# A pooling layer's norms: mean-and-variance instruction per half, residual added on VectorE, residual rows and weight splits in other places

## The chip, the cores and the metric

One core of a Trainium2 chip runs the whole network in one launch. The metric is the device time of one execution in microseconds. TensorE does the matmuls, ScalarE (ACT) and VectorE (DVE) the elementwise work, GpSimd (POOL) here only powers of single columns, SyncE (SP) issues the transfers of weights. Each engine works its own instructions in the order in which they stand, and waits for the others by semaphores.

## What is computed

A two-layer transformer block is followed by a second block, on 256 tokens of width 1024. Layer 0 is attention, layer 1 a pooling mixer; each is followed by a layer norm, a gated feed-forward and another layer norm. The change lies where layer 0 ends and layer 1 begins:

```python
def multiscale_pool(h, w_pool, pool_scale):
    ...                                   # windowed means over 2, 4, 8, 16 tokens, minus h
    pooled = jnp.stack(outs, axis=2).astype(h.dtype)
    y = jnp.einsum('bsgi,gio->bsgo', pooled, w_pool).reshape(B, S, D)
    return y * pool_scale
...
        hx = modulate(x, sh1, sc1)
        ...
            y_lat = multiscale_pool(hx, pool_w[p], pool_scale[p])
        x = layer_norm(ALPHA * x + g1 * y_lat, ln_g[i, 0], ln_b[i, 0])
        x = layer_norm(ALPHA * x + g2 * swiglu(modulate(x, sh2, sc2), ffn_w_in[i], ffn_w_out[i]),
                       ln_g[i, 1], ln_b[i, 1])
```

## The kernel before

The 256 tokens are two halves, t = 0 and 1, of 128 rows each. Weights come as blocks of 128 x 1024 values in a fixed plan. SyncE loads up to 11 blocks ahead. For a precise product each block is split: ScalarE writes `hi`, the block rounded (L285), VectorE writes `lo`, what is left (L291), and TensorE does three matmuls, hi by the high part of the activations `xTh`, lo by `xTh`, hi by the low part `xTl` (L376 to L378). Eight `hi`/`lo` pairs can be held; `st.step(n)` splits up to n blocks of the plan where it stands, as long as seven are not yet passed, `st.pump()` as many as fit. The two blocks `PW` of the pooling weights are used whole.

The order is that of the program text; no scheduler moves anything. Around the pooling layer it runs so:

- `ffn(0, ...)` ends with the output product of half 0 and `ac0(0)`, then `mid_pool`, then the output product of half 1 and `ac0(1)`. `ac0` calls `ln_out`: VectorE multiplies the product by a row and adds the residual `xa` (L871, L872, sums taken along), ScalarE squares for the variance (L875), VectorE takes the power's argument (L418), GpSimd the power (L420), and VectorE writes the pooling input `hx` (L894, L898). `pooled` (L1119) multiplies by the window matrix; `keep(KW["a"])` puts five filler matmuls (L216) between its two token halves.
- `mid_pool` and later `ln_norm` normalise the rows on ScalarE (L905), and `next_xa` makes from them the next residual `xa` on VectorE (L910, L912).
- `res(t)` adds `xa` into PSUM by two matmuls with the identity (L1159), before the pool product for half 0, after it for half 1. `pool_mm` is the product with `PW` (L1186).
- `ln_core(0)`: ScalarE copies the sum out of PSUM with its row sum (L880), squares (L882), VectorE normalises (L890); `next_xa(1)` stands in between. `tr_evac` transposes (L722), ScalarE scales (`tev`, L745) and writes `xTh` (L425), VectorE `xTl` (L426).
- `ln_core(1)` follows, then layer 1's feed-forward. Its first chunk takes blocks G0 to G3 for both halves' gate and U0 to U3 for the other factor. TensorE does G for half 0, then U for half 0; after the sixth of U's eight steps come the transposes of half 1, then the rest.

`PS = (2, 2, 3, 3)` says how many blocks are taken at four places: in `mid_pool` (both are `PW`), after the pooled sums are copied out, before `tr_evac` and after it.

## Time and profile before

| | |
|---|---|
| median of 3 runs | 1149.41 us (1147.62 to 1149.92) |
| the profiled execution's own time | 1149.09 us |
| its span, first to last instruction | 1147.2 us |
| TensorE busy | 1110.0 us (97%) |
| VectorE, ScalarE, GpSimd busy | 759.9, 557.4, 22.6 us |
| TensorE's granted clock, mean | 0.996 of 2.4 GHz |
| the stage of the change | about 420 to 455 us |

A busy TensorE here mostly means matmuls that follow each other without a gap. What a change is worth is read at the places where TensorE stands: its timeline shows a gap in brackets with the engine that ended it, and the timelines of the other engines show what that engine did meanwhile.

### The profile page before, as it was taken

Reading aid. Unit: us, or ns where it says so; the run is one execution under the profiler, and the core shown is the slowest. Engines: PE = TensorE matmul, PEld = TensorE weight load, DVE = VectorE, ACT = ScalarE, POOL = GpSimd, SP = SyncE. Lnnn points to the kernel's source line nnn. Section 1 sums busy time; section 2 is a strip of 40 time slices with the busy share of each in tenths; the row PEclk is TensorE's granted clock in tenths of the full one; section 3 lists DMA queues with packets and bytes.
Section 4 is the critical chain, followed back from the end, with each engine's and each line's share of the span. In section 5 each row is a group of like instructions: output and inputs, shape, how many; then the busy total and the mean of one; then the engine's idle time right before and its main releaser. Section 6 shows DMA issues by size and latency. Waiting matters only on the chain.

```text
span 1147.2 us, 14156 instructions
## 1 busy us (share of the span) xinstructions
PE 1110.0 (97%) x5186; PEld 880.4 (77%) x5186; DVE 759.9 (66%) x1114; ACT 557.4 (49%) x913; POOL 22.6 (2%) x35
## 2 busy tenths in 40 slices
PE   7999888999999999999999999999999999999998
PEld 3578665678888776888888688887778877888887
DVE  7984967669986865577455865545636776555465
ACT  3452456454444427534443765557226355445353
POOL 0000000000000000000000110000000000000000
PEclk9999999999999999999999999999999999999999
DMA  9973741569997926568464654553434646464611
GB/s 360 359 261 116 275 147 60 195 233 372 343 419 280 332 79 220 191 215 303 168 225 146 224 196 147 189 193 126 169 108 146 208 147 210 162 212 164 207 38 37
DMA packets 65922, 234.62 MB, mean 205 GB/s; under 512 B 7323, under 2 KB 8347, under 8 KB 65852
## 3 DMA queue, kind: packets, MB, share of 16 engines
q1 hardware_dynamic: 64080, 227.97, 55.9%
q10 hardware_dynamic: 1772, 5.74, 1.5%
q8 instruction: 41, 0.67, 0.2%
q14 instruction: 29, 0.24, 0.1%
HBM read 232.63 MB, written 1.05 MB: 204 GB/s over the span
## 4 chain that ended last, share of the span: by engine, by line
PE 79%; DVE 10%; ACT 4%; issue 3%; DMA 2%; POOL 0%; SPq 0%; ACTq 0%; POOLq 0%; DVEq 0%
PE mm L378 16%; PE mm L376 16%; PE mm L377 16%; PE big L390 12%; PE big L392 6%; DVE lo L291 3%; DMA raw<-in_dram 2%; DVE junkb L526 2%; DVE raw L269 1%; PE big L384 1%; DVE st L666 1%; PE big L404 1%; PE big L405 1%; PE big L403 1%; PE tr L981 1%
## 5 line engine op out<-in xcount | busy, mean ns | idle before, releaser
L291 DVE TENSOR_TENSOR lo<-raw,hi 128x1024 fp32r<-128x1024 f32 x316 | 374.5, 1221 | 133.1 <-ACT hi L285 129.6
L285 ACT ACTIVATE hi<-raw 128x1024 fp32r<-128x1024 f32 x316 | 321.5, 1056 | 70.7 <-PE mm L378 52.2
L376 PE MATMUL mm<-hi,xTh 128*128 128x512 f32 (+1 forms) x872 | 337.6, 387 | 2.8 <-ACT xTh L425 2.7
L377 PE MATMUL mm<-lo,xTh 128*128 128x512 f32 (+1 forms) x872 | 331.8, 380 | 2.0 <-DVE lo L291 1.3
L378 PE MATMUL mm<-hi,xTl 128*128 128x512 f32 (+1 forms) x872 | 332.2, 381 | 0.6 <-DVE xTl L738 0.4
L376 PEld LDWEIGHTS mm<-hi,xTh 128*128 128x128 f32 x872 | 164.1, 188 | 38.4 <-ACT xTh L425 4.6
L378 PEld LDWEIGHTS mm<-hi,xTl 128*128 128x128 f32 x872 | 164.0, 188 | 34.1 <-DVE xTl L426 1.9
L377 PEld LDWEIGHTS mm<-lo,xTh 128*128 128x128 f32 x872 | 164.2, 188 | 33.4 <-DVE lo L291 3.6
L269 DVE SCALAR_TENSOR_TENSOR raw<-raw,crow 128x1024 f32<-128x1024 f32 x80 | 96.8, 1219 | 0.0
L390 PE MATMUL big<-hi,hh 128*128 128x512 f32 x256 | 80.6, 396 | 0.0
L390 PE MATMUL big<-lo,hh 128*128 128x512 f32 x256 | 79.2, 391 | 0.0
L392 PE MATMUL big<-hi,hl 128*128 128x512 f32 x256 | 79.0, 390 | 0.0
L425 ACT ACTIVATE hh<-tr 128x512 fp32r<-128x512 f32 (+1 forms) x40 | 22.9, 575 | 89.6 <-PE tr L981 49.2
L961 ACT ACTIVATE h<-mm 128x512 f32<-128x512 f32 (+1 forms) x24 | 13.5, 561 | 91.6 <-PE mm L378 91.6
L392 PEld LDWEIGHTS big<-hi,hl 128*128 128x128 f32 x256 | 48.0, 188 | 10.3
L390 PEld LDWEIGHTS big<-lo,hh 128*128 128x128 f32 x256 | 48.0, 188 | 10.3
L426 DVE TENSOR_TENSOR hl<-tr,hh 128x512 fp32r<-128x512 f32 (+1 forms) x40 | 26.3, 662 | 44.0 <-ACT hh L425 43.2
L390 PEld LDWEIGHTS big<-hi,hh 128*128 128x128 f32 x256 | 46.7, 188 | 8.6
L420 POOL TENSOR_TENSOR st<-st,half 128x4 f32<-128x4 f32 (+1 forms) x28 | 21.7, 776 | 1029.0 <-DVE st L418 1015.9
L1607 DVE TENSOR_TENSOR h<-h 128x512 f32<-128x512 f32 x16 | 11.0, 689 | 33.8 <-ACT h L1606 33.7
L1606 ACT ACTIVATE h<-mm 128x512 f32<-128x512 f32 x16 | 9.6, 598 | 39.8 <-PE mm L378 39.8
L667 ACT ACTIVATE p<-big,st 128x512 f32<-128x512 f32 x16 | 11.0, 689 | 31.4 <-DVE st L666 31.4
(316 smaller groups left out, 1256.2 us busy)
## 6 DMA issues: line engine op xcount, KB each, us to landing
raw<-in_dram SPq DMA_DIRECT2D x426, 512.0 KB, 5.0
row<-in_dram ACTq DMA_DIRECT2D x8, 512.0 KB, 6.2
tok<-in_dram SPq DMA_DIRECT2D x8, 256.0 KB, 8.0
xa<-in_dram SPq DMA_DIRECT2D x2, 512.0 KB, 6.6
out_dram<-sg SPq DMA_DIRECT2D x3, 256.0 KB, 2.0
pmat<-in_dram ACTq DMA_DIRECT2D x1, 544.0 KB
crow<-in_dram ACTq DMA_DIRECT2D x1, 512.0 KB, 6.4
out_dram<-sg SPq DMA_DIRECT2D x2, 128.0 KB, 1.7
```

The source lines that it names most:

```text
L269: V.scalar_tensor_tensor(raw, raw, 1.0, crow, op0=OP.mult, op1=OP.mult, accum_out=mc[l][:, nb:nb + 1])
L285: A.activation(hi, raw, AF.Copy)
L291: V.tensor_tensor(lo, raw, hi.bitcast(F32), op=OP.subtract)
L376: TE.matmul(ps, h, hi[:, sl], start=s, stop=False)
L377: TE.matmul(ps, h, lo[:, sl], start=False, stop=False)
L378: TE.matmul(ps, l, hi[:, sl], start=False, stop=e)
L390: TE.matmul(halves[f], h, w[:, f * 512:(f + 1) * 512], start=first and b == 0, stop=False)
L392: TE.matmul(halves[f], l, hi[:, f * 512:(f + 1) * 512], start=False, stop=last)
L420: G.tensor_tensor(r, v, half_e[:, :w], op=OP.pow)
L425: A.activation(dh, ps, AF.Copy)
L426: V.tensor_tensor(dl, ps, dh.bitcast(F32), op=OP.subtract)
L526: V.scalar_tensor_tensor(junk, raws[b], 1.0, crow if s_ else ccrow, op0=OP.mult, op1=OP.mult, accum_out=acc[2 * s_ + b])
```

## The change

- In `ac0(1)`, `ln_bn` takes the place of `ln_out`'s sums and square: after multiply and add, BN_STATS on each 512 columns and one BN_AGGR give mean and variance on VectorE. The filler is three matmuls instead of five.
- `res` is gone. VectorE adds `xa` while it reads the pool product from PSUM: for half 0 in `ln_bn(0)`, for half 1 in `ln_p` (with sums, the square still on ScalarE). ScalarE's copy with a row sum (L880) and its normalising pass (`ln_norm`, L905) are gone.
- The residual rows come from `xa_two`: two VectorE steps from the unnormalised rows, mean and power, with the two rows scaled by ALPHA on ScalarE beforehand (in `mid_gb`). Half 0's stand after the pooled sums are copied out, half 1's after the transposes of half 0.
- `PS = (3, 0, 2, 0)`: `mid_pool` splits G0; `hi_only(3)` has ScalarE write the high parts of G1 to G3 after the pooled sums are copied out, and `lo_only(1)` puts VectorE's part of each at three places: in the power's wait, after the first and after the second transposed half of half 0. The three transfers that follow are issued after the third. U0 and U1 are split before `ln_core(1)`, U2 and U3 after it.
- The normalising step of half 0 is done in two halves of 512 columns, each transposed by itself; of the scaling of four transposed columns two are on ScalarE and two on VectorE. Three of the four pooled sums are copied out by ScalarE.

```diff
-PS = (2, 2, 3, 3)
+PS = (3, 0, 2, 0)
-KW = dict(a=5, b=0, c=0)
+KW = dict(a=3, b=0, c=0)
...
+        def hi_only(self, n):
+            for _ in range(n):
+                it, raw = self.take()
+                self.split(it[1], raw, (0,))
+                self.pend.append((it[1], raw, self.his))
+
+        def lo_only(self, n):
+            for _ in range(n):
+                key, raw, self.his = self.pend.pop(0)
+                self.split(key, raw, (1,))
+                if not self.pend:
+                    self.dma()
...
     def ln_p(t, ps):
-        A.activation(s[t], ps, AF.Identity, accum_out=sm[:, 0:1])
-        V.tensor_scalar(sm[:, 1:2], sm[:, 0:1], -1.0 / D, None, op0=OP.mult)
+        for f in range(2):
+            V.scalar_tensor_tensor(s[t][:, fs], ps[:, fs], 1.0, xa[t][:, fs], op0=OP.mult, op1=OP.add,
+                                   accum_out=sm[:, f:f + 1])
+        V.tensor_scalar(sm[:, 1:2], sm[:, 0:1], sm[:, 1:2], -1.0 / D, op0=OP.add, op1=OP.mult)
         A.activation(ps, s[t], AF.Square, bias=sm[:, 1:2], accum_out=sm[:, 2:3])
+    def ln_bn(t, ps, grow=None):
+        b6 = bp.t([P, 2, 6], "bn6", bufs=2)
+        for f in range(2):
+            if grow is None:
+                V.tensor_tensor(s[t][:, fs], ps[:, fs], xa[t][:, fs], op=OP.add)
+            else:
+                V.tensor_tensor(s[t][:, fs], ps[:, fs], grow[:, fs], op=OP.mult)
+                V.tensor_tensor(s[t][:, fs], s[t][:, fs], xa[t][:, fs], op=OP.add)
+            V.bn_stats(out=b6[:, f], in_=s[t][:, fs])
+        V.bn_aggr(out=mv_[:, 0:2], in_=b6)
+    def xa_two(t, mean, r, rows, op, part):
+        if part == 0:
+            V.scalar_tensor_tensor(xa[t], s[t], mean, rows[0], op0=op, op1=OP.mult)
+        else:
+            V.scalar_tensor_tensor(xa[t], xa[t], r, rows[1], op0=OP.mult, op1=OP.add)
...
     def mid_gb():
+        for r in nx["rows"][:2]:
+            A.activation(r, r, AF.Copy, scale=ALPHA)
...
     def mid_pool():
-        ln_norm(0, mrs[0])
-        next_xa(0, nx["rows"])
         st.step(PS[0])
...
-    res(0)
-            if g % 2 == 0:
+            if g != 1:
                 A.activation(dst, pv, AF.Copy)
-    st.step(PS[1])
-    ln_norm(1, mrs[1])
-    cur["rows"] = ln_rows(2, ALPHA)
+    st.hi_only(3)
+    for part in range(2):
+        xa_pool(0, part)
     pps.append(big())
...
     pool_mm(0)
     pool_mm(1)
-    ln_core(0, pps[0], None, lambda: next_xa(1, rows1))
-    res(1)
+    m0 = ln_bn(0, pps[0])
+    r0 = rstd(m0[:, 1:2], 1, LN_EPS, 1)
+    st.lo_only(1)
+    for f in range(2):
+        V.tensor_scalar(s[0][:, fs], s[0][:, fs], m0[:, 0:1], r0, op0=OP.subtract, op1=OP.mult)
+    for f in range(2):
+        tr_half(s[0][:, 512 * f:512 * f + 512], f, 0, xTh, xTl, cur["cols"], fp, act_t=(0, 1))
+        st.lo_only(1)
     st.done(("PW", 0), ("PW", 1))
+    for part in range(2):
+        xa_pool(1, part)
+    cur["rows"] = ln_rows(2, ALPHA)
     st.step(PS[2])
-    tr_evac(s[0], 0, xTh, xTl, cur["cols"], fp)
-    st.step(PS[3])
     ln_core(1, pps[1], None)
```

On VectorE, from the normalising step of half 0 (L890 before) to the fourth U block, the order before was this. The `lo` rows are G2, G3, U0, then U1, U2, then U3; L881 to the second L890 is the layer norm of half 1:

```order
L890 TENSOR_SCALAR s_1326<-s_1326,st_816_3560,st_818_3568 128x1024 [waits Pool_49]
L291 TENSOR_TENSOR lo_3575<-raw_3257,hi_3573 128x1024 [waits DMAHW1_49,Activation_49]
L291 TENSOR_TENSOR lo_3581<-raw_3263,hi_3579 128x1024 [waits DMAHW2_49,Activation_49]
L291 TENSOR_TENSOR lo_3587<-raw_3266,hi_3585 128x1024 [waits DMAHW3_49,Activation_49]
L426 TENSOR_TENSOR xTl_71<-tev_3596,xTh_70 128x4x128 [waits Activation_49]
L426 TENSOR_TENSOR xTl_71<-tev_3608,xTh_70 128x4x128 [waits Activation_49]
L291 TENSOR_TENSOR lo_3617<-raw_3272,hi_3615 128x1024 [waits DMAHW4_49,Activation_49]
L291 TENSOR_TENSOR lo_3623<-raw_3275,hi_3621 128x1024 [waits DMAHW5_49,Activation_49]
L881 TENSOR_SCALAR st_838_3627<-st_838_3627 128x1 [waits Activation_49]
L418 TENSOR_SCALAR st_839_3631<-st_838_3627 128x1 [waits Activation_49]
L890 TENSOR_SCALAR s_1326<-s_1326,st_838_3627,st_840_3633 128x1024 [waits Pool_49]
L291 TENSOR_TENSOR lo_3684<-raw_3281,hi_3682 128x1024 [waits DMAHW6_49,Activation_49]
```

And in the changed kernel, from the lo of G3 to that of U3 (L293 is a lo, L920 and L922 the residual of half 1, L898 to L929 the layer norm of half 1):

```order
L293 TENSOR_TENSOR lo_3591<-raw_3265,hi_3529 128x1024 [waits DMAHW2_49]
L920 SCALAR_TENSOR_TENSOR xa_1325<-s_1326,st_803_3501,row_2512 128x1024
L922 SCALAR_TENSOR_TENSOR xa_1325<-xa_1325,st_805_3505,row_2514 128x1024 [waits DVE_49]
L293 TENSOR_TENSOR lo_3607<-raw_3268,hi_3605 128x1024 [waits DMAHW3_49,Activation_49]
L293 TENSOR_TENSOR lo_3613<-raw_3274,hi_3611 128x1024 [waits DMAHW4_49,Activation_49]
L898 SCALAR_TENSOR_TENSOR s_1326,st_835_3617<-big_3533,xa_1325 128x512 [waits DVE_49]
L898 SCALAR_TENSOR_TENSOR s_1326,st_835_3617<-big_3533,xa_1325 128x512
L900 TENSOR_SCALAR st_835_3617<-st_835_3617 128x1 [waits DVE_49]
L434 TENSOR_SCALAR st_836_3622<-st_835_3617 128x1 [waits Activation_49]
L929 TENSOR_SCALAR s_1326<-s_1326,st_835_3617,st_837_3624 128x1024 [waits Pool_49]
L293 TENSOR_TENSOR lo_3629<-raw_3277,hi_3627 128x1024 [waits DMAHW5_49,Activation_49]
L293 TENSOR_TENSOR lo_3681<-raw_3283,hi_3679 128x1024 [waits DMAHW6_49,Activation_49]
```

The residual steps and two splits now stand ahead of that layer norm, and the lo of U2 stands behind its normalising step instead of ahead of it.

On TensorE, the matmuls on U2 for half 0 (the 37th to the 42nd of the feed-forward) and the first transpose of half 1, before:

```order
L376 MATMUL mm_3663<-hi_3621,xTh_70 128x512 [waits Activation_49]
L377 MATMUL mm_3663<-lo_3623,xTh_70 128x512 [waits DVE_49]
L378 MATMUL mm_3663<-hi_3621,xTl_71 128x512
L376 MATMUL mm_3663<-hi_3621,xTh_70 128x512
L377 MATMUL mm_3663<-lo_3623,xTh_70 128x512
L378 MATMUL mm_3663<-hi_3621,xTl_71 128x512
L722 MATMUL tr_3688<-cst_72,s_1326 128x128 [waits DVE_49]
```

and now:

```order
L392 MATMUL mm_3660<-hi_3627,xTh_70 128x512 [waits Activation_49]
L393 MATMUL mm_3660<-lo_3629,xTh_70 128x512 [waits DVE_49]
L394 MATMUL mm_3660<-hi_3627,xTl_71 128x512
L392 MATMUL mm_3660<-hi_3627,xTh_70 128x512
L393 MATMUL mm_3660<-lo_3629,xTh_70 128x512
L394 MATMUL mm_3660<-hi_3627,xTl_71 128x512
L738 MATMUL tr_3685<-cst_72,s_1326 128x128 x4
```

The waits for U2's two parts stand at the same matmuls; the transposes no longer have a wait of their own, since the lo that was waited for stands behind the normalising step.

On VectorE around the pool product's statistics, the order before, from the last copied pooled sum to the normalising step:

```order
L1170 COPY pw_805_3519<-big_3478 128x512 [waits Activation_49]
L291 TENSOR_TENSOR lo_3526<-raw_3196,hi_3524 128x1024 [waits DMAHW7_49,Activation_49]
L291 TENSOR_TENSOR lo_3532<-raw_3254,hi_3530 128x1024 [waits DMAHW0_49,Activation_49]
L904 TENSOR_TENSOR st_812_3536<-st_800_3493,st_802_3503 128x1
L881 TENSOR_SCALAR st_816_3560<-st_816_3560 128x1 [waits Activation_49]
L910 SCALAR_TENSOR_TENSOR xa_1325<-s_1326,row_2512 128x1024
L912 SCALAR_TENSOR_TENSOR xa_1325<-row_2514,xa_1325 128x1024 [waits DVE_49]
L418 TENSOR_SCALAR st_817_3566<-st_816_3560 128x1 [waits Activation_49]
L890 TENSOR_SCALAR s_1326<-s_1326,st_816_3560,st_818_3568 128x1024 [waits Pool_49]
```

And now, from the first residual step of half 0 to the first scaled column of half 0:

```order
L920 SCALAR_TENSOR_TENSOR xa_1325<-s_1326,st_790_3407,row_2512 128x1024
L922 SCALAR_TENSOR_TENSOR xa_1325<-xa_1325,st_792_3417,row_2514 128x1024 [waits DVE_49]
L909 TENSOR_TENSOR s_1326<-big_3518,xa_1325 128x512 [waits DVE_49,PE_49]
L913 BN_STATS bn_813_3550<-s_1326 128x6 [waits DVE_49]
L909 TENSOR_TENSOR s_1326<-big_3518,xa_1325 128x512
L913 BN_STATS bn_813_3550<-s_1326 128x6 [waits DVE_49]
L915 BN_AGGR st_814_3555<-bn_813_3550 128x2 [waits DVE_49]
L434 TENSOR_SCALAR st_815_3557<-st_814_3555 128x1 [waits DVE_49]
L293 TENSOR_TENSOR lo_3561<-raw_3256,hi_3525 128x1024 [waits DMAHW0_49,Activation_49]
L1242 TENSOR_SCALAR s_1326<-s_1326,st_814_3555,st_816_3559 128x512 [waits Pool_49]
L1242 TENSOR_SCALAR s_1326<-s_1326,st_814_3555,st_816_3559 128x512
L763 TENSOR_SCALAR tev_3570<-tr_3565,Gc_3302,Bc_3303 128x128 [waits PE_49,Activation_49]
```

The sums and squares that L881 and L418 waited for on ScalarE are VectorE's own (L909 to L915); G0's and G1's splits are out of the stretch ahead, and one lo stands in the power's wait.

## Rows read from the trace of the kernel before

**Rows 1.** Busy time by stretch, from 455 us on.
```profile
455.00:1147.00 692.00, 683.37 (x3244) 558.98 (x3244) 407.58 (x528) 341.04 (x543) 15.03 (x20) 1.00 0.50 171
```

**Rows 2.** TensorE timeline: start us, us, engine, line, operation, count, [idle before <- releaser].
```profile
421.79 4.46 PE L216 MATMUL tr<-crow 128*128 128x512 f32 x10
426.14 1.19 PE L1119 MATMUL mm<-pmat,pw 128*128 128x136 f32 x8
...
428.10 1.88 PE L1159 MATMUL big<-xa,cst 128*128 128x512 f32 x4
429.81 7.07 PE L1186 MATMUL big<-raw,pw 128*128 128x256 f32 x32
...
439.11 1.04 PE L722 MATMUL tr<-cst,s 128*128 128x128 f32 x8
441.97 0.50 PE L376 MATMUL mm<-hi,xTh 128*128 128x512 f32 x1 [1.82 <-ACT xTh L425]
...
442.89 0.50 PE L378 MATMUL mm<-hi,xTl 128*128 128x512 f32 x1 [0.20 <-DVE xTl L426]
...
452.12 1.03 PE L722 MATMUL tr<-cst,s 128*128 128x128 f32 x8
...
454.97 0.50 PE L376 MATMUL mm<-hi,xTh 128*128 128x512 f32 x1 [0.45 <-ACT xTh L425]
```

**Rows 3.** VectorE timeline, same columns.
```profile
417.26 1.23 DVE L910 SCALAR_TENSOR_TENSOR xa<-s,row 128x1024 f32<-128x1024 f32 x1 [1.39 <-ACT s L905]
...
420.14 0.69 DVE L871 TENSOR_TENSOR s<-big,row 128x512 f32<-128x512 f32 x1 [0.39 <-PE big L405]
420.86 0.69 DVE L872 SCALAR_TENSOR_TENSOR s<-s,xa 128x512 f32<-128x512 f32 x1
...
425.33 1.41 DVE L898 SCALAR_TENSOR_TENSOR pw<-pw,st,row 128x512 f32<-128x512 f32 x2 [0.72 <-POOL st L420]
...
436.01 1.22 DVE L912 SCALAR_TENSOR_TENSOR xa<-row,xa 128x1024 f32<-128x1024 f32 x1
437.15 0.15 DVE L418 TENSOR_SCALAR st<-st 128x1 f32<-128x1 f32 x1
438.02 0.81 DVE L890 TENSOR_SCALAR s<-s,st,st 128x1024 f32<-128x1024 f32 x1 [0.72 <-POOL st L420]
438.75 3.49 DVE L291 TENSOR_TENSOR lo<-raw,hi 128x1024 fp32r<-128x1024 f32 x3
442.15 0.69 DVE L426 TENSOR_TENSOR xTl<-tev,xTh 128x512 fp32r<-128x512 f32 x1
...
444.95 2.36 DVE L291 TENSOR_TENSOR lo<-raw,hi 128x1024 fp32r<-128x1024 f32 x2 [0.26 <-ACT hi L285]
...
449.50 0.81 DVE L890 TENSOR_SCALAR s<-s,st,st 128x1024 f32<-128x1024 f32 x1 [0.66 <-POOL st L420]
```

**Rows 4.** ScalarE timeline, same columns, from two windows.
```profile
366.73 0.60 ACT L425 ACTIVATE hh<-tr 128x512 fp32r<-128x512 f32 x1 [2.23 <-PE tr L981]
...
439.75 1.50 ACT L745 ACTIVATE tev<-tr,Bc,Gc 128x128 f32<-128x128 f32 x4 [0.79 <-PE tr L722]
441.28 0.63 ACT L425 ACTIVATE xTh<-tev 128x512 fp32r<-128x512 f32 x1
...
447.41 1.12 ACT L882 ACTIVATE big<-s,st 128x1024 f32<-128x1024 f32 x1 [0.55 <-DVE st L881]
```

**Rows 5.** Groups by line and shape: count | busy us, mean ns | idle before.
```profile
L1340 DVE SCALAR_TENSOR_TENSOR sc<-c2d,tr 128x128 f32<-128x128 f32 x8 | 1.8, 281 | 0.1
```

**Rows 6.** Stretches: us, engines' busy us, TensorE's granted clock, DMA share, GB/s.
```profile
410.00:420.00 10.00, 10.00 (x46) 8.29 (x45) 7.56 (x13) 2.49 (x3) 0.54 (x1) 1.00 0.00 1
155.80:159.50 3.70, 0.03 (x2) 0.02 (x1) 3.42 (x11) 1.21 (x3) 1.02 (x1) 1.00 0.75 247
160.70:164.20 3.50, 3.50 (x14) 2.68 (x16) 1.70 (x5) 2.77 (x8) 0.00 (x0) 0.51 0.70 275
86.00:89.00 3.00, 2.86 (x9) 2.50 (x10) 3.00 (x4) 1.54 (x2) 0.00 (x0) 0.50 0.80 289
```

More of the change, by code (lines that the diff above doesn't have):

```diff
@@ L246, in __init__ @@
             self.raws, self.tiles = {}, {}
+            self.pend = []
             self.mods_done = set()
@@ L265, in emit @@
         def emit(self):
+            assert not self.pend
             it, raw = self.take()
@@ L294, in split @@
             assert self.nw <= self.ndone + R, key
+        def hi_only(self, n):
+            for _ in range(n):
+                it, raw = self.take()
+                assert it[0] == "w" and not is32(it[1])
+                self.split(it[1], raw, (0,))
[6 more added lines that the diff above has]
+                    self.dma()
         def prescale(self, key, raw=None):
@@ L717, in body, with tr_half @@
     o32 = bp.t([P, 4, T], "pw0")
-    def tr_half(src, f, t, dh, dl, cols=None, pool=None, scalars=None, f32=False):
+    def tr_half(src, f, t, dh, dl, cols=None, pool=None, scalars=None, f32=False, act_t=ACT_T):
         ps = trt()
@@ L743, in tr_half @@
             k = 4 * f + j
-            if j in ACT_T:
+            if j in act_t:
                 A.activation(tmp[:, j], pv[:, j], AF.Identity, scale=gc[:, k:k + 1], bias=bc[:, k:k + 1])
@@ L900, in ln_out @@
         return sm[:, 1:2], r
-    def ln_norm(t, mr):
-        nmr = small(1)
-        V.tensor_tensor(nmr, mr[0], mr[1], op=OP.mult)
-        A.activation(s[t], s[t], AF.Identity, scale=mr[1], bias=nmr)
     def next_xa(t, rows, parts=(0, 1)):
@@ L1123, in f, with xa_pool @@
         def f(ps):
-            if t == 1:
-                pooled(0, range(8))
-                keep(KW["a"])
-            mrs[t] = ln_out(t, ps, nx["g2"], hx[t], nx["G"], nx["B"],
-                            lambda f: pooled(1, range(4 * f, 4 * f + 4)) if t == 1 else None)
-        return f
+            if t == 0:
+                mrs[0] = ln_out(0, ps, nx["g2"], hx[0], nx["G"], nx["B"]) + (OP.add,)
+                return
+            pooled(0, range(8))
+            keep(KW["a"])
+            m = ln_bn(1, ps, nx["g2"])
+            r = rstd(m[:, 1:2], 1, LN_EPS, 1)
+            V.scalar_tensor_tensor(hx[1], s[1], m[:, 0:1], nx["G"], op0=OP.subtract, op1=OP.mult)
+            for f in range(2):
+                fs = slice(f * 512, f * 512 + 512)
+                V.scalar_tensor_tensor(hx[1][:, fs], hx[1][:, fs], r, nx["B"][:, fs], op0=OP.mult, op1=OP.add)
+                pooled(1, range(4 * f, 4 * f + 4))
+            mrs[1] = (m[:, 0:1], r, OP.subtract)
+        return f
+    def xa_pool(t, part):
+        mean, r, op = mrs[t]
+        xa_two(t, mean, r, nx["rows"], op, part)
     def mid_pool():
-        ln_norm(0, mrs[0])
-        next_xa(0, nx["rows"])
         st.step(PS[0])
@@ L1154, in body @@
     pps = [big()]
-    def res(t):
-        for f in range(2):
-            fs = slice(f * 512, f * 512 + 512)
-            TE.matmul(pps[t][:, fs], ident, xa[t][:, fs], start=t == 0, stop=t == 1, skip_group_check=True)
-    res(0)
     p32 = [bp.t([P, 4, T], f"pw{i}") for i in range(2)]
@@ L1172, in body @@
             split_evac(pv, xTh[:, 2 * g:2 * g + 2], xTl[:, 2 * g:2 * g + 2])
-    st.step(PS[1])
-    ln_norm(1, mrs[1])
-    rows1 = nx["rows"]
-    cur["rows"] = ln_rows(2, ALPHA)
-    cur["cols"] = nx["cols"]
+    st.hi_only(3)
+    for part in range(2):
+        xa_pool(0, part)
     pps.append(big())
@@ L1186, in pool_mm @@
                     TE.matmul(pps[t][:, g * T:(g + 1) * T], p32[g // 2][:, g % 2 * 2 + k, t * P:(t + 1) * P], w[:, o_:o_ + T],
-                              start=t == 1 and g % 2 == 0 and k == 0, stop=t == 0 and k == 1, skip_group_check=True)
+                              start=k == 0, stop=k == 1)
                 continue
@@ L1199, in body @@
     pool_mm(1)
-    ln_core(0, pps[0], None, lambda: next_xa(1, rows1))
-    res(1)
+    m0 = ln_bn(0, pps[0])
+    r0 = rstd(m0[:, 1:2], 1, LN_EPS, 1)
+    st.lo_only(1)
+    for f in range(2):
+        fs = slice(f * 512, f * 512 + 512)
+        V.tensor_scalar(s[0][:, fs], s[0][:, fs], m0[:, 0:1], r0, op0=OP.subtract, op1=OP.mult)
+    cur["cols"] = nx["cols"]
+    for f in range(2):
+        tr_half(s[0][:, 512 * f:512 * f + 512], f, 0, xTh, xTl, cur["cols"], fp, act_t=(0, 1))
+        st.lo_only(1)
     keep(KW["b"])
     st.done(("PW", 0), ("PW", 1))
+    for part in range(2):
+        xa_pool(1, part)
+    cur["rows"] = ln_rows(2, ALPHA)
     st.step(PS[2])
-    tr_evac(s[0], 0, xTh, xTl, cur["cols"], fp)
-    st.step(PS[3])
     ln_core(1, pps[1], None)
```

4 lines of the change are left out of this document (added).

## The prediction

> **What bounds the kernel now.** I read the stages first (busy time by stretch), then TensorE's timeline from 420 to 455 us, then VectorE's and ScalarE's over the same stretch, each time looking for the wait that ends last. From 455 us to the end TensorE is busy 683.37 of 692 us [rows 1]: a delay that exists at 455 us stays to the end, and so does a gain. So the change is worth whatever it does to one instant, the matmul at 454.97 us with which the first feed-forward chunk of layer 1 turns to token half 1 [rows 2]. In what follows G0 to G3 and U0 to U3 are the eight weight blocks of that chunk; a block needs a high part from ScalarE and a low part ("lo") from VectorE, and TensorE takes it with six matmuls for each token half. 40 of these matmuls lie between 442.89 and 452.12 us [rows 2], 0.231 us each.
>
> What is to be seen in the rows before the change: TensorE stands between 440 and 441.97 us for the transposed rows of half 0, and hardly afterwards. It asks for the lo of U2 (its 38th matmul) at 442.89 + 35 x 0.231 = 451.0 us, and VectorE has had it since 444.95 + 2.36 = 447.3 us [rows 2, 3]. VectorE did U1 and U2 before the last steps of half 1's layer norm, whose normalising step is at 449.50 us. That is 3.7 us of slack, and it is what I think the change spends.
>
> **The change part by part.** Times are on the clock of the trace. "Dependent" VectorE instructions of 512 columns start 0.72 us apart (420.14 and 420.86), independent ones 0.66 (two in 1.41, the later one lasting 0.75); a lo takes 3.49 / 3 = 1.16 [rows 3].
>
> *Costing nothing.* Scaling two rows by ALPHA on ScalarE (two passes of 1024 columns, at most 1.12 us each as the square) lies in the 2.23 us that ScalarE idles before 366.73 us [rows 4]; without that cover it would push back the evacuation that follows by 2.2 us. The split of G0 takes the place of the old normalising pass and residual row of half 0, in the idle time around 417.26 us [rows 3]. The late issue of three weight transfers (after the third lo) hides too: the queue is idle from 410 to 420 us, with the eleven blocks ahead landed [rows 6]. The wait for the first later block is on the pooled matmuls, which come sooner. Shortening the filler matmuls (4.46 us for ten pieces, now six pieces) gives nothing: TensorE then waits longer for the same VectorE result.
>
> *Statistics of half 1 in the last layer norm of layer 0.* VectorE now does per half: multiply, add, BN_STATS, then BN_AGGR and the small step. BN_STATS has no row. Ends: 0.40 us (a single-operand pass of 1024 columns takes 0.81 [rows 3], half of it) and 1.22 us (a 1024-column pass, as if it read twice [rows 3]). I take 0.69, one pass of 512, since it reads 512 numbers as the add in front of it does. 420.14 + 4.26 (six instructions, one of them independent, five dependent) + 0.4 (two small ones) + 1.28 (the first write of the pooling input) = 426.05 us where the scaling started at 425.33 before [rows 3]: **0.7 us late**. The old square on ScalarE was hidden by that first write, so taking it away returns nothing.
>
> *Pooling.* The second set of pooled matmuls starts at 426.14 + 0.7 = 426.85 and is done 1.96 later, 428.8 [rows 2]. The residual matmuls (1.88 us) no longer stand ahead of the pool product, so this starts at 428.8 instead of 429.81 us. Its first half, 7.07 / 2, ends at 432.4: **1.0 us early** [rows 2]. VectorE is free by then: copying one pooled group (from about 428) and the two residual steps of half 0 (1.22 each [rows 3]) end near 431.1.
>
> *Statistics of half 0.* The order shows one wait on TensorE for both halves, so the adds start at 432.5: 2.8 (add, BN_STATS, add, BN_STATS) + 0.35 (two small) = 435.7; the lo of G1 (1.16) covers the power on GpSimd (437.15 to 438.02 before, 0.87 [rows 3]) and ends at 436.85; two normalising halves 0.81 [rows 3] end at 437.25 and 437.65. The transposes start at 437.35 instead of 439.11 [rows 2], and 0.64 later ScalarE evacuates two of four columns (half of 1.50 [rows 4], 438.8). VectorE's two columns wait for ScalarE's (its wait list in the order shows it), about 0.28 each by a 128-column row [rows 5]: 439.35; xTh 0.63 [rows 4]: 440.0. The feed-forward's first matmul is at about **440.05 instead of 441.97**, its third at 440.75 instead of 442.89. That gain is 1.9 to 2.1 us and holds only while blocks keep coming.
>
> *The queue behind it.* VectorE is in order. After xTl of half 0 (0.69 [rows 3], to 440.65) stand: lo G2, 441.8; two columns, 442.3; xTh of half 1, 442.95; xTl, 443.6; lo G3, 444.75; two residual steps of half 1 (1.22 each), 447.15; lo U0, **448.3**. TensorE asks for it at 440.75 + 23 x 0.231 = 446.05: 2.2 us of wait, and the early start is spent. Then lo U1, 449.45; two adds with sums, 450.85; a small one, 451.05; the square on ScalarE (1.12 [rows 4], with its sum 1.3), 452.35; the power, 453.2; normalise 0.81, 454.0; and only then **lo U2, 455.2**. TensorE asks for it at 448.3 + 12 x 0.231 = 451.1 and waits 4.1 us. ScalarE is behind in the same way: the high part of U2 now stands behind the square. Five more matmuls, and the transposes of half 1 start at 455.2 + 5 x 0.231 = 456.35 instead of 452.12 [rows 2]: **4.2 us late**. From there to the matmul that stood at 454.97 nothing changes: U3's lo is there at 456.4, and the transposed rows take as long as before.
>
> *The clock.* After TensorE stood from 155.80 to 159.50 us (0.03 of 3.70 busy), the granted clock was 0.51 from 160.70 to 164.20, and 0.50 again from 86.00 to 89.00 [rows 6], that is 1.2 of 2.4 GHz. The stretch from 451.1 to 455.2 holds one matmul. If the clock falls behind it, the rows at half speed last about 3.3 us, of which some 2.4 fall on work that runs: 1.2 us lost. Ends: 0 and half of 3.5, 1.75. A fall before the first matmul at 440.05 (only transposes from 435.9 on) would be taken up by the wait for U0.
>
> Sum: 4.2 + 1.2 = 5.4 us. The profiled execution took 1149.09 us (a span of 1147.2 and 1.9 around it), the median of the runs is 1149.41; so 1154.5 on the first and **1154.8 us** on the second. BN_STATS at its ends moves this by 4 x (0.40 - 0.69) = -1.2 and 4 x (1.22 - 0.69) = +2.1.
>
> One rule speaks for a little less. The rows show a dependent pair 0.06 us further apart than an independent one [rows 3]. The Trainium skill, page "VectorE: DVE Perf Modes", section "The DRAIN you can't avoid", states that a semaphore between two VectorE instructions costs nothing extra. By it the eight dependent hand-overs in the two statistics chains would give back 0.5 us, 1154.3; by the rows the sum stands, and I keep it.
>
> **The rivals.**
> *The clock holds.* Only the 4.2 us: **1153.6 us**. For it: between 440 and 441.97 us TensorE also stood, and the matmuls behind ran at their old spacing [rows 2]. Against it: the new stand is twice as long.
> *VectorE gets there sooner (no change).* If the adds of half 0 may start when the first half of the pool product is written (1.8 us sooner) and BN_STATS costs 0.40, the lo of U2 comes at 452.2: +1.2 and no fall of the clock, **1150.6 us**. Against it: the order gives the second add no wait of its own, so the first one's wait covers both.
> *Faster: the early start is kept.* The chain through the pool lost 1.88 us of residual matmuls and ScalarE's two passes over the rows, and the feed-forward starts 1.9 us sooner (3.1 with BN_STATS at its low end): **1146.3 to 1147.5 us**. It decides if the lo of U2 is there by 440.75 + 35 x 0.231 = 448.8 us, so VectorE would have to need 6.4 us less than I add up between 432.5 and 455.2; no single row is that far off.
> *The change does not do what it says* is excluded for the order (it is built so), and open for BN_STATS alone: at 1.22 it gives 1156.9.
>
> **How the numbers follow.** Clock falls, 1154.8: 0.45. Clock holds, 1153.6: 0.30. No change, 1150.6: 0.14. Faster, 1146.9: 0.11. Within 0.2% (about what a measurement of this kernel can tell from no change) is 1147.1 to 1151.7. Faster 0.11, same 0.14, slower 0.75. The likeliest's own range is 1153.6 to 1156.9. For 8 in 10 the range reaches down through the no-change case to 1150.0 and up to 1157.5 (BN_STATS dear and the clock loss 1.75); outside are the faster case and some 0.08 at the two ends.
>
> **What would show it.** Right, on TensorE's timeline: the first matmul of layer 1's feed-forward about 2 us earlier, a wait of about 2 us on a lo after 25 matmuls, one of about 4 us on a lo after 37, transposes of half 1 about 4 us later, and the same spacing from there to the end; on VectorE: the normalising step of half 1 ahead of U2's lo; in the clock of the stretches behind 454 us: 0.5 for some 3 us. Wrong: BN_STATS far from 0.69 us; no wait on U2; a later stage that gives the 4 us back; or TensorE's work between 420 and 455 us ending sooner than 455.

## The result and the profile after

The changed kernel takes **1162.59 us** (median of 4 runs, 1161.51 to 1163.23) against 1149.66 us before in the same session: ratio 1.0114 (95% interval 1.0101 to 1.0127), some 13 us slower. The forecast was 1154.8 us with a range up to 1157.5: right in sign, too small by more than half. The profiled execution has a span of 1160.0 us.

VectorE's timeline after, first. Columns in all timelines: start us, duration us, engine, line, operation, out<-in, shapes, count, [idle before <- releaser].

```profile
423.52 0.69 DVE L913 BATCH_NORM_STATS2 bn<-s 128x6 f32<-128x512 f32 x1
424.25 0.21 DVE L915 BATCH_NORM_AGGREGATE st<-bn 128x2 f32<-128x12 f32 x1
424.50 0.15 DVE L434 TENSOR_SCALAR st<-st 128x1 f32<-128x1 f32 x1
424.57 1.27 DVE L1167 SCALAR_TENSOR_TENSOR pw<-s,st,row 128x1024 f32<-128x1024 f32 x1
426.28 1.42 DVE L1170 SCALAR_TENSOR_TENSOR pw<-pw,st,row 128x512 f32<-128x512 f32 x2 [0.44 <-POOL st L436]
...
432.70 0.69 DVE L909 TENSOR_TENSOR s<-big,xa 128x512 f32<-128x512 f32 x1 [1.18 <-PE big L1223]
433.42 0.69 DVE L913 BATCH_NORM_STATS2 bn<-s 128x6 f32<-128x512 f32 x1
434.03 0.67 DVE L909 TENSOR_TENSOR s<-big,xa 128x512 f32<-128x512 f32 x1
...
435.71 0.15 DVE L434 TENSOR_SCALAR st<-st 128x1 f32<-128x1 f32 x1
435.79 1.23 DVE L293 TENSOR_TENSOR lo<-raw,hi 128x1024 fp32r<-128x1024 f32 x1
437.45 1.00 DVE L1242 TENSOR_SCALAR s<-s,st,st 128x512 f32<-128x512 f32 x2 [0.43 <-POOL st L436]
...
446.04 1.28 DVE L920 SCALAR_TENSOR_TENSOR xa<-s,st,row 128x1024 f32<-128x1024 f32 x1
447.36 1.28 DVE L922 SCALAR_TENSOR_TENSOR xa<-xa,st,row 128x1024 f32<-128x1024 f32 x1
448.56 2.35 DVE L293 TENSOR_TENSOR lo<-raw,hi 128x1024 fp32r<-128x1024 f32 x2
...
454.63 0.81 DVE L929 TENSOR_SCALAR s<-s,st,st 128x1024 f32<-128x1024 f32 x1 [0.72 <-POOL st L436]
455.36 2.35 DVE L293 TENSOR_TENSOR lo<-raw,hi 128x1024 fp32r<-128x1024 f32 x2
```

This is the queue as the prediction had laid it out: the residual passes of half 1 (446.04, 447.36) stand ahead of the lo of U0 and U1, and the lo of U2 comes behind half 1's normalising step, where before it was done 2.2 us ahead of it (444.95 + 2.36 against 449.50) [rows 3]. The waits of 0.44 and 0.43 us for GpSimd (426.28, 437.45) stand where before had 0.72 each [rows 3]; the forecast had hidden both behind work on VectorE, and they come back below.

TensorE's timeline after, and what ScalarE does ahead of U2's high part (the row 453.63). They answer to [rows 2, 4].

```profile
421.68 2.74 PE L216 MATMUL tr<-crow 128*128 128x512 f32 x6
427.08 1.19 PE L1155 MATMUL mm<-pmat,pw 128*128 128x136 f32 x8 [2.66 <-DVE pw L1170]
...
429.04 7.07 PE L1223 MATMUL big<-raw,pw 128*128 128x256 f32 x32
438.06 1.20 PE L738 MATMUL tr<-cst,s 128*128 128x128 f32 x8 [1.94 <-DVE s L1242]
441.09 0.79 PE L392 MATMUL mm<-hi,xTh 128*128 128x512 f32 x1 [1.84 <-ACT xTh L441]
...
449.83 0.50 PE L393 MATMUL mm<-lo,xTh 128*128 128x512 f32 x1 [0.60 <-DVE lo L293]
...
454.72 0.51 PE L392 MATMUL mm<-hi,xTh 128*128 128x512 f32 x1 [2.08 <-ACT hi L287]
456.63 0.80 PE L393 MATMUL mm<-lo,xTh 128*128 128x512 f32 x1 [1.41 <-DVE lo L293]
...
458.93 1.91 PE L738 MATMUL tr<-cst,s 128*128 128x128 f32 x8
```
```profile
452.48 1.12 ACT L901 ACTIVATE big<-s,st 128x1024 f32<-128x1024 f32 x1 [5.94 <-DVE st L900]
...
453.63 1.04 ACT L287 ACTIVATE hi<-raw 128x1024 fp32r<-128x1024 f32 x1
```

Feed-forward starts a little sooner, then TensorE waits at U0's lo, 3.5 us at U2 (first for the high part, which stands behind the square on ScalarE, then for the lo), and the transposes of half 1 come late. The rows 449.83 and 456.63 are the two forecast waits. The granted clock in the stretches around (window, length, busy us of PE, PEld, DVE, ACT, POOL, then PEclk, DMA share, GB/s; as [rows 6]):

```profile
440.00:444.00 4.00, 2.91 (x7) 2.29 (x8) 2.79 (x6) 1.69 (x4) 0.00 (x0) 0.50 0.25 83
...
446.00:450.00 4.00, 3.40 (x16) 2.50 (x15) 3.96 (x5) 0.54 (x1) 0.00 (x0) 1.00 0.99 331
450.00:456.00 6.00, 3.15 (x12) 2.00 (x12) 3.87 (x9) 3.52 (x5) 0.54 (x1) 1.00 0.58 193
456.00:462.00 6.00, 5.37 (x17) 4.49 (x18) 1.71 (x2) 2.04 (x6) 0.00 (x0) 0.50 0.54 175
462.00:464.00 2.00, 2.00 (x9) 1.60 (x8) 0.69 (x1) 1.97 (x6) 0.00 (x0) 0.79 0.00 0
```

Two falls to 1.2 GHz: one behind the stands around 437 to 441 us, one in the wait for U2, at half for all of 456 to 462.

The table puts the stage of all kernels on one zero, the start of the filler matmuls (L216; 421.79 before, 421.68 after), whose place against the matmuls ahead of it is the same in all. "38th" is the matmul on U2's first lo, "end mark" the matmul that stood at 454.97 before [rows 2].

| us from the filler | pool product | first FFN matmul | 38th | transposes half 1 | end mark |
|---|---|---|---|---|---|
| before | 8.02 | 20.18 | 29.19 | 30.33 | 33.18 |
| predicted | 7.01 | 18.26 | 33.41 | 34.56 | 38.58 |
| after | 7.36 | 19.41 | 34.95 | 37.25 | 41.36 |
| after, second profile (r_after) | 7.36 | 19.41 | 34.93 | 37.23 | 40.55 |
| e_u2 | 7.36 | 19.40 | 30.99 | 34.94 | 38.87 |
| e_fill | 7.36 | 19.41 | 36.03 | 37.18 | 40.04 |
| e_pow | 7.36 | 18.54 | 34.08 | 35.93 | 39.25 |
| e_xa | 7.37 | 19.42 | 32.44 | 33.69 | 36.55 |
| v_order | 8.85 | 19.90 | 28.67 | 29.81 | 32.66 |
| v_half1 | 6.24 | 17.30 | 26.09 | 27.23 | 30.08 |

So the stage lost 41.36 - 33.18 = 8.2 us (7.4 in the second profile), not 5.4. One profile is not the kernel, though: in b_shift, b_256 and b_64, where the stage's instructions are those of before, the end mark stands at 34.75 to 34.77, because the clock falls to 0.57 from 444 to 448 us (b_256) where it holds at 1.00 in before. A figure of this table can be off by 1.6 us for that reason alone.

The remaining 4 to 5 us are lost where the change touches no instruction. Aligned row by row, TensorE's lag is +7.9 us at 513 and +12.4 at 1090 us (1.0 of that is a fall of the clock near 782 us that the second profile doesn't have). It also grows by 0.85 us from 269 to 389 us, ahead of the stage. The groups of matmuls whose stationary operand (the one loaded into TensorE ahead of the matmul, behind the comma in the rows) is the feed-forward's hidden tile show it, before and then after (count | busy us, mean ns | idle):

```profile
L390 PE MATMUL big<-hi,hh 128*128 128x512 f32 x256 | 80.6, 396 | 0.0
L390 PE MATMUL big<-lo,hh 128*128 128x512 f32 x256 | 79.2, 391 | 0.0
L392 PE MATMUL big<-hi,hl 128*128 128x512 f32 x256 | 79.0, 390 | 0.0
```
```profile
L406 PE MATMUL big<-hi,hh 128*128 128x512 f32 x256 | 82.0, 401 | 0.0
L406 PE MATMUL big<-lo,hh 128*128 128x512 f32 x256 | 80.4, 395 | 0.0
L408 PE MATMUL big<-hi,hl 128*128 128x512 f32 x256 | 80.3, 394 | 0.0
```

The same source lines, the same shapes, 4 to 5 ns longer each. What changed about them is an address: the two small BN_STATS buffers (48 bytes each, 128 bytes with padding) stand ahead of the hidden tiles in on-chip memory and push them from multiples of 256 bytes (204032, 206080, ...) to 128 above (204160, 206208, ...), as the built programs place them. The transposed input xTh lies elsewhere and didn't move.

### The profile page after: what moved, and what is told of

Same layout as the page of the kernel before. It is cut to its first block, busy times and chain, and to the rows that moved or that the text cites. A ratio compares the mean times of both kernels' runs of the same rounds, so it can differ in the third digit from the quotient of the medians.

```text
span 1160.0 us, 14138 instructions
## 1 busy us (share of the span) xinstructions
PE 1116.6 (96%) x5174; PEld 883.1 (76%) x5174; DVE 766.3 (66%) x1124; ACT 552.0 (48%) x902; POOL 24.5 (2%) x35
## 3 DMA queue, kind: packets, MB, share of 16 engines
HBM read 232.63 MB, written 1.05 MB: 201 GB/s over the span
## 4 chain that ended last, share of the span: by engine, by line
PE 79%; DVE 11%; ACT 3%; issue 3%; DMA 2%; POOL 1%; SPq 0%; ACTq 0%; POOLq 0%; DVEq 0%
PE mm L394 16%; PE mm L392 16%; PE mm L393 16%; PE big L406 12%; PE big L408 6%; DVE lo L293 3%; DVE junkb L542 2%; DMA raw<-in_dram 2%; DVE raw L271 1%; PE big L400 1%; DVE st L682 1%; PE big L420 1%; PE tr L738 1%; PE big L421 1%; PE big L419 1%
## 5 line engine op out<-in xcount | busy, mean ns | idle before, releaser
L293 DVE TENSOR_TENSOR lo<-raw,hi 128x1024 fp32r<-128x1024 f32 x316 | 374.6, 1220 | 133.8 <-ACT hi L287 131.6
L406 PEld LDWEIGHTS big<-lo,hh 128*128 128x128 f32 x256 | 48.2, 188 | 11.5
L408 PEld LDWEIGHTS big<-hi,hl 128*128 128x128 f32 x256 | 48.1, 188 | 11.5
L1003 DVE TENSOR_TENSOR h<-h,mm 128x512 f32<-128x512 f32 (+1 forms) x24 | 15.3, 639 | 16.3 <-PE mm L394 16.3
```

Of the source, the lines that this page charges most:

```text
L293: V.tensor_tensor(lo, raw, hi.bitcast(F32), op=OP.subtract)
L406: TE.matmul(halves[f], h, w[:, f * 512:(f + 1) * 512], start=first and b == 0, stop=False)
L408: TE.matmul(halves[f], l, hi[:, f * 512:(f + 1) * 512], start=False, stop=last)
```

## The experiments

The e_ and v_ kernels are edits of the kernel after, the b_ kernels of the kernel before. Ratios are to before, timed beside each.

**Before and after again (r_before, r_after).**

> The kernel before, unchanged, once more with a profile on the chip on which the others of this set run. In the two profiles so far the spacing of equal matmuls is 227.4 ns before and up to 230.6 ns after, also in stretches that the change does not touch. If that belongs to the chip or the moment, this run's spacing is as the changed kernel's beside it and its time is nearer to 1152 us; if it belongs to the change (its tiles lie 128 bytes further on), this run shows 227.4 ns and 1149.4 us.

> The changed kernel, unchanged, on the same chip. By the theory that the loss is in one stage, the matmul with which the feed-forward turns to half 1 is 8.1 us later than in the run of before beside it, and the rest of the 13 us is a spacing of matmuls (about 3.6 us) and one fall of the clock near 790 us (1.1 us) that need not come back. By the rival that the change costs all 13 us, the lag still grows after 465 us against the run beside it.

1150.00 us, ratio 1.0001 (0.9992 to 1.0011), and 1163.38 us, 1.011 (1.0095 to 1.0125). The mean start-to-start distance of matmuls from 300 to 350 us, ahead of the stage, is again 227.4 ns before and 230.5 ns after. So the wider spacing belongs to the change and not to one chip or one run.

**The lo of U2 ahead of half 1's sums (e_u2).**

```
-PS = (3, 0, 2, 0)
+PS = (3, 0, 3, 0)
```

> The changed kernel with three blocks instead of two split ahead of the layer norm of half 1, so that U2 stands ahead of it. Theory (VectorE's queue sets the end: the lo of U2 waits behind a layer norm): TensorE no longer waits for U2, but the layer norm comes 1.15 us later, its normalising step ends near 456.6 us instead of 455.4, and the transposes of half 1 follow it at 456.7 instead of 458.9: 2 us faster than the changed kernel, and more if the clock does not fall. Rival (the falls of the clock alone make the loss): the wait for U2 goes and the time falls by over 5 us.

1161.07 us, ratio 1.0092 (1.0076 to 1.0109), 2.3 us under r_after by the medians; the intervals overlap, so the stage has to show it. The 38th matmul stands 3.9 us sooner, and then TensorE waits for the normalising step that the lo delays:

```profile
458.88 1.79 PE L738 MATMUL tr<-cst,s 128*128 128x128 f32 x8 [2.65 <-DVE s L929]
```

The transposes gain 2.3 us. The work on VectorE is the same in either order; moving one piece moves the wait to the next.

**Fillers in the two stands (e_fill).**

```
     pool_mm(1)
+    keep(2)
...
-                do_u(0, 0, {XR[l]: x1_ready})
+                do_u(0, 0, {XR[l]: x1_ready, **({4: lambda: keep(4)} if l == 1 else {})})
```

> The changed kernel with filler matmuls (two after the pool product, four ahead of the matmuls on U2) in the two stands of TensorE; no other work is touched. Theory: the clock stays at 2.4 GHz and the loss by its second fall (6.2 us of work at half speed, 3.1 us) comes back: 2.5 to 3 us faster than the changed kernel, with the first matmul behind the wait for U2 still at about 456.6 us. Rival (the queue alone sets the time, the slow matmuls are hidden): no change within 0.5 us.

1161.29 us, ratio 1.0096 (1.0081 to 1.0111), 2.1 us under r_after by the medians where 2.5 to 3 were expected; here too the intervals overlap. The clock was not kept throughout: with the first stand filled it falls later, when TensorE waits 1.97 us for U0's lo (to 450.50). The matmuls behind that wait run slowly, the fillers come late and delay the 38th matmul by 1.1 us. But behind the fillers the clock is whole (the stretch ahead of them is not):

```profile
452.00:455.00 3.00, 3.00 (x10) 2.33 (x9) 1.17 (x6) 1.85 (x3) 0.28 (x1) 0.67 0.86 288
455.00:467.00 12.00, 11.57 (x47) 7.76 (x46) 5.06 (x6) 5.93 (x13) 0.26 (x1) 1.00 0.28 95
```

From the 38th matmul to the end mark it takes 40.04 - 36.03 = 4.0 us, as before (3.99); after, 6.4 and 5.6. That difference, **1.6 to 2.4 us, is what the second fall costs**.

**Placement (b_shift, e_align, b_256, b_64).** b_shift is the kernel before with one unused tile of 128 bytes, b_256 and b_64 the same with 256 and 64:

```
     o32 = bp.t([P, 4, T], "pw0")
+    G.memset(bp.t([P, 32], "pad2"), 0.0)
```

e_align is the kernel after with each statistics buffer enlarged to 128 bytes:

```
-        b6 = bp.t([P, 2, 6], "bn6", bufs=2)
+        b6 = bp.t([P, 32], "bn6", bufs=2)[:, :12].rearrange("p (f c) -> p f c", f=2)
```

> The kernel before with one unused tile of 128 bytes per partition added in front of the tiles that the change's two small statistics buffers push up, and a memset of it at the start of the program on GpSimd; nothing else differs. Every tile behind it (the FFN's hidden tiles among them) moves from an address that is a multiple of 256 bytes to one that is 128 above. Theory of placement: the pitch of matmuls whose stationary operand lies in a moved tile goes from 227-228 to 231-234 ns as in the kernel after, that of matmuls on the unmoved transposed input stays 227, and the time rises by 3.5 to 4.5 us over 1150.0 (ratio 1.003 to 1.004). Rival: the wider pitch of the kernel after comes from its instructions (a different mix of work on the other engines); then the pitch stays 227.4 and the time within 1 us of 1150.

> The kernel after with each of the two statistics buffers made 128 bytes per partition (of which the first 48 are used), so that the tiles behind them lie 256 bytes higher than before and again on multiples of 256. Theory of placement: the mean pitch between 300 and 350 us returns from 230.5 to 227.4 ns, and the time falls by 3.5 to 4.5 us from 1163.4 to 1159-1160; what is left over before, 9 to 10 us, is then the pooling stage's and the clock's. Rival (instructions): no change, 1163.4.

> The kernel before with an unused tile of 256 bytes per partition at the place where the run with 128 had its own, and the same memset: everything behind it moves by 256 bytes and stays on multiples of 256. Theory of placement (what counts is the address within 256 bytes): the pitch between 300 and 350 us is 227.4 ns and the time that of before, 1149.7, within 1 us. Rival (the extra tile, its memset or the longer distance cost the time): 1154 to 1155.5, as with 128 bytes.

> The same with a tile of 64 bytes: everything behind it stands 64 above a multiple of 256. Theory of placement: a pitch of 230 to 231 ns between 300 and 350 us as with 128 bytes, time 1154 to 1155.5. Rival (only the half of 256, or nothing below 128, counts): pitch 227.4 and 1149.7.

| | hidden tiles above a multiple of 256 | ns, 300 to 350 us | us | ratio |
|---|---|---|---|---|
| b_shift | 128 | 230.6 | 1155.15 | 1.0049 (1.0037 to 1.0062) |
| b_64 | 64 | 230.9 | 1157.12 | 1.0063 (1.0051 to 1.0075) |
| b_256 | 0 | 227.4 | 1149.79 | 1.0000 (0.9992 to 1.0008) |
| e_align | 0 | 227.4 | 1158.52 | 1.0080 (1.0065 to 1.0095) |

The rows of b_256 and then of b_shift, from 300 to 400 us, with one group on the unmoved input as control:

```profile
L378 PE MATMUL mm<-hi,xTl 128*128 128x512 f32 x74 | 28.8, 389 | 0.0
...
L390 PE MATMUL big<-hi,hh 128*128 128x512 f32 x48 | 15.3, 399 | 0.0
...
L392 PE MATMUL big<-hi,hl 128*128 128x512 f32 x46 | 14.2, 390 | 0.0
```
```profile
L378 PE MATMUL mm<-hi,xTl 128*128 128x512 f32 x72 | 28.0, 390 | 0.0
...
L390 PE MATMUL big<-hi,hh 128*128 128x512 f32 x48 | 15.5, 405 | 0.0
...
L392 PE MATMUL big<-hi,hl 128*128 128x512 f32 x47 | 14.8, 395 | 0.0
```

A tile of 256 bytes costs nothing, 128 or 64 bytes cost 5.6 and 7.2 us (b_shift was expected at 3.5 to 4.5): what counts is the address within 256 bytes, not the tile, its memset or the distance. In the kernel after, placement is worth 1.0110 - 1.0080 = 3.4 us by the ratios (4.9 by the medians); e_align's profile holds one more fall of the clock, in the pooled matmuls of half 1, which take 2.13 us instead of 1.19, and its pool product stands 9.03 us from the filler instead of 7.36:

```profile
426.18 2.13 PE L1155 MATMUL mm<-pmat,pw 128*128 128x136 f32 x8 [2.67 <-DVE pw L1170]
```

The lag row by row gives it without that fall: leaving out the stage and the fall near 782 us, TensorE's lag in after grows by 0.9 us from 250 to 375, 1.25 from 475 to 775 and 3.0 from 800 to 1125 us, **5.1 us** in all, and that of e_align in the same stretches by nothing (it stays at 7.9 and then 8.3). Some 1100 matmuls of 512 columns have a stationary operand in a moved tile and came about 5 ns further apart in b_shift (768 and 144 in the feed-forward, about 190 on the tiles obT and qkd): 1100 x 5 ns = 5.5 us. Transposes of 128 columns on moved tiles stayed at 108 to 109 ns. Why 64 costs more than 128, if it does, isn't settled: the intervals overlap.

**The residual rows out of the chain (e_xa).** Half 0's two passes go ahead of half 1's statistics, those of half 1 take their old place:

```
     def mid_pool():
         st.step(PS[0])
+        for part in range(2):
+            xa_pool(0, part)
...
     st.hi_only(3)
     for part in range(2):
-        xa_pool(0, part)
+        xa_pool(1, part)
...
     st.done(("PW", 0), ("PW", 1))
-    for part in range(2):
-        xa_pool(1, part)
```

> The kernel after with the residual rows of half 0 (two VectorE passes of 1.28 us) moved ahead of the statistics of half 1, where VectorE has a wait for the FFN's last sums, and those of half 1 put in the place of half 0's, so that no residual pass stands between the pooling's half 0 and the lower splits. Theory of the VectorE queue: 2.56 us leave the queue behind the transposes of half 0; the lower split of U0 and U1 end 2.6 us sooner, U0's wait (0.60 us) goes, the transposes of half 1 stand up to 2.6 us sooner, and the time falls by 2.5 to 4 us (more if the shorter stand keeps the clock at 1.00). Rival: the stand is set by the square of half 1 on ScalarE behind its U splits, or by U2's transfer, and the time falls by under 1 us.

1158.58 us, ratio 1.0081 (1.0066 to 1.0097): 3.3 us by the ratios, 4.8 by the medians. The 38th matmul stands 2.5 us sooner (the two passes are 2.56), the clock holds behind it, and one wait of 1.41 us for U2's lo is left:

```profile
454.82 0.50 PE L393 MATMUL mm<-lo,xTh 128*128 128x512 f32 x1 [1.41 <-DVE lo L293]
```

**No VectorE work beside the power (e_pow).** The lo of G1 goes from ahead of the two normalising passes to behind them.

> The kernel after with the one lower split that runs on VectorE during the power on GpSimd (half 0 of the pooling) moved behind the two normalising passes. Theory (the two engines slow each other): the power takes 0.54 us instead of 1.41, as where VectorE waits for it, the normalising passes begin 0.8 us sooner and the first FFN matmul stands 0.7 to 0.8 us sooner, at a stream that is late behind it anyway, so the end moves by under 1 us. Rival: the power's 1.41 us are its own at this place, and nothing moves but the split.

GpSimd's power and the normalising passes in e_pow, then the two powers of after (the passes that follow are its 426.28 and 437.45):

```profile
438.30 0.54 POOL L436 TENSOR_TENSOR st<-st,half 128x1 f32<-128x1 f32 x1 [9.76 <-DVE st L434]
```
```profile
438.88 1.00 DVE L1241 TENSOR_SCALAR s<-s,st,st 128x512 f32<-128x512 f32 x2 [0.72 <-POOL st L436]
```
```profile
424.73 1.52 POOL L436 TENSOR_TENSOR st<-st,half 128x1 f32<-128x1 f32 x1 [10.76 <-DVE st L434]
...
436.01 1.41 POOL L436 TENSOR_TENSOR st<-st,half 128x1 f32<-128x1 f32 x1 [9.77 <-DVE st L434]
```

0.54 us alone, 1.41 beside the lo. From the small step ahead of the power to the normalising passes it takes 0.88 us (438.00 to 438.88) instead of 1.74 (435.71 to 437.45); the first FFN matmul gains 0.87 us. The time is 1161.06 us, 1.0100 (1.0083 to 1.0116): the interval overlaps that of after, so only the stage shows it. There the 38th matmul gains the same 0.87 us, though the lo is still to be done: the queue behind is bound by VectorE, and VectorE lost 0.87 us waiting.

**The queue laid out anew (v_order, v_half1).** v_order, on e_align: residual rows as in e_xa, five high parts made early on ScalarE, no lo beside the power, transposed columns all on ScalarE, half 1's sums behind the lo of U0 with those of U1 and U2 in the wait for its square, and one filler. Each of these lo also issues one transfer of its own (not shown below), where after issues three behind the third:

```
+    st.hi_only(5)
+    for part in range(2):
+        xa_pool(1, part)
...
     pool_mm(1)
+    keep(1)
+    st.lo_only(1)
     m0 = ln_bn(0, pps[0])
...
+    st.lo_only(2)
+    tr_half(s[0][:, 0:512], 0, 0, xTh, xTl, cur["cols"], fp)
+    st.lo_only(1)
+    tr_half(s[0][:, 512:1024], 1, 0, xTh, xTl, cur["cols"], fp)
+    st.hi_only(2)
     st.done(("PW", 0), ("PW", 1))
+    ln_core(1, pps[1], None, lambda: st.lo_only(2))
+    st.lo_only(1)
```

v_half1 is v_order with the statistics of half 1 ahead of the pooling taken as before (sums on VectorE, square on ScalarE) and keep(4) in the wait for them.

> The kernel after with its buffers back on multiples of 256 bytes and the queues of the pooling stage laid out anew: residual rows of half 0 ahead of half 1's statistics, those of half 1 in their place; the upper halves of five splits made early on ScalarE; the lower half of G1 in VectorE's wait for the pooling's sums and none beside the power; all transposed columns scaled on ScalarE; half 1's sums taken after U0's lower split, those of U1 and U2 in the wait for its square; one filler behind the pooling's matmuls. Theory (the stage is bound by VectorE's queue, then by the clock): the first FFN matmul stands 20.1 us behind the last FFN matmul ahead of the stage (after 21.10, before 21.87), none of the next 43 matmuls waits, the transposes of half 1 stand at 30.2 to 30.5 (after 38.9, before 32.0), and the time is 1148 to 1149.5, at or just under before's 1150. Rival (each shift of this stage makes the clock fall somewhere else in it): 2 to 4 us are lost to a half clock, 1150.5 to 1153.

> The same, with the statistics of half 1 ahead of the pooling (not those of the pooling itself) taken as in the kernel before, with the square on ScalarE, and one filler more in the wait for them. Theory: before's form puts the pooling's second half at 6.04 us behind the last FFN matmul, the mean-and-variance instructions beside a slow power (1.52 us) at 7.09, so this is 1.05 us sooner: first FFN matmul at 19.0, time 1147 to 1148.5. Rival: the stage is bound by VectorE's queue, which the form of the statistics does not shorten, and the time is that of the order without it, within 0.3 us.

v_order: 1148.55 us (11 runs), ratio 0.9995 (0.9986 to 1.0004). v_half1: **1147.33 us** (11 runs), 0.9985 (0.9976 to 0.9993), about 1.7 us faster than before; both times lie where they were expected. TensorE and VectorE in v_half1:

```profile
424.99 1.19 PE L1154 MATMUL mm<-pmat,pw 128*128 128x136 f32 x8 [0.68 <-DVE pw L936]
...
438.00 0.50 PE L391 MATMUL mm<-hi,xTh 128*128 128x512 f32 x1 [1.74 <-ACT xTh L440]
...
447.93 1.03 PE L737 MATMUL tr<-cst,s 128*128 128x128 f32 x8
```
```profile
442.11 2.35 DVE L293 TENSOR_TENSOR lo<-raw,hi 128x1024 fp32r<-128x1024 f32 x2
...
445.25 0.81 DVE L928 TENSOR_SCALAR s<-s,st,st 128x1024 f32<-128x1024 f32 x1 [0.72 <-POOL st L435]
```

The lo of U1 and U2 now lie in the wait for the square (442.11), the normalising step at 445.25 is done 1.9 us before the transposes at 447.93 want it, and no matmul between 438.00 and 447.93 waits. v_order's end mark is worse by 2.6 us, more than the 1.05 us that were expected of half 1's statistics, because its clock falls behind the wait ahead of the pooled matmuls, as in e_align (0.57 from 426 to 430 us in both):

```profile
426.75 2.18 PE L1154 MATMUL mm<-pmat,pw 128*128 128x136 f32 x8 [2.66 <-DVE pw L1169]
```

This fall also puts its first FFN matmul 1.5 us later than expected (19.90 from the filler; v_half1's 17.30 is where it was expected), as its rival had it, though not the time (1150.5 or more) that went with it. In after the same wait of 2.66 us brought no fall (1.00 from 426 to 431). In the medians 1.2 us are left of the 2.6, which fits a fall that not every run has; this was not shown.

## Why the prediction was wrong

Two steps failed. "The same spacing from there to the end" put the cost of everything behind the stage at nothing without a reason, and it cost about 5 us. In the stage, where the mechanism was right, the lo of G1 did not cover the power, and the loss by the clock was taken too small.

**The edits that cost nothing**: right as far as the runs show, for r_after's lag behind r_before grows by 1.0 us from 250 to 400 us, as much as b_shift's behind before, which is the placement alone. The shorter filler is not always free: it leaves the stand of 2.66 us ahead of the pooled matmuls, and where the clock fell behind it the pool product stands at 9.03 (e_align) and 8.85 (v_order) instead of 7.36.

**Memory was no step at all**: the prediction took the rows from 455 us on as fixed ("the same spacing from there to the end") and didn't ask what the new buffers displace. This is the larger miss: 5.1 us by the lag in after, 3.4 by e_align's ratio, 5.6 by b_shift's. None of the rivals held it.

**Statistics of half 1**: right in kind, short by 0.35 us. BN_STATS takes 0.69 us, the value taken. The first write of the pooling input ends at 425.84, sooner than the 426.05 of the sum, but it does not cover the power, which takes 1.52 us beside it; so the scaling starts at 426.28. From the filler that is 1.06 us later than before, and 0.7 were forecast. v_half1 shows that this form has a price: the pooled matmuls of half 1 stand 5.40 us from the filler after, 4.28 there.

**Pooling**: the same 0.35 us late (7.36 against 7.01), else right.

**Statistics of half 0**: the sums start at 432.70 (forecast 432.5), but the step "the lo of G1 covers the power" failed. The power does not run under the lo but behind it, so the two take 1.66 us (435.79 to 437.45), more than the power's 0.87 or the lo's 1.16: the normalising passes begin at 437.45, not 436.85, and last 1.00, not 0.81. With the columns split between two engines the first FFN matmul is at 441.09, 1.04 us later than forecast; e_pow gives 0.87 of that back.

**The queue behind it**: right in order and mechanism, mis-sized by what it inherits. U0's lo is late by 1.5 us more than forecast (449.83 for 448.3), the 38th matmul by 1.5 (34.95 for 33.41): 0.9 from the power, the rest from small terms: two columns on VectorE take 0.72 us, the wait for xTh behind them 0.76 and a residual step 1.28, where the sum had 0.5 to 0.56, 0.63 to 0.65 and 1.22. The 38th matmul is 5.8 us late where the sum had 4.2. e_xa and v_order confirm that this is VectorE's queue: shortening it or laying its waits elsewhere moves the 38th matmul by as much.

**The clock**: it falls, as forecast, and the first fall is absorbed by the wait for U0, as forecast (of its 2.2 us 0.60 are left, at 449.83). The second cost 2.4 us in after, where the clock is at 0.51 from 456 to 463 us, and 1.6 in r_after, where it is at 0.57 from 457 to 461; 1.2 was taken and 1.75 was the end, from stretches of some 3.5 us [rows 6]. That bound came from the two falls that the profile of before happened to hold; r_before holds a longer one, at 0.51 from 159 to 166 us. It was also chance that the profile of before holds no fall behind the old stand at 440 us, on which the rival "the clock holds" leaned; b_256's has one.

**The rule of the Trainium skill** ("VectorE: DVE Perf Modes", "The DRAIN you can't avoid"), by which the hand-overs were free: the rows here do not bear it out. An add's statistics start 0.72 us behind it (432.70, 433.42), the next, independent add 0.61 behind those (434.03). The rows were the better guide.

**The rivals** fall with this: the clock does not hold (1153.6), BN_STATS is neither 0.40 nor 1.22 us (1150.6, 1156.9). The faster one (1146.3 to 1147.5) asked for a VectorE that needs several us less ahead of U2's lo; the kernel after does not do that, v_half1 does, at 1147.33.

**The sum**: 5.8 (queue) + 1.6 to 2.4 (clock) + 5.1 (placement) = 12.5 to 13.3 us; measured 12.9, with an interval from 11.6 to 14.6.
